# Attention scores: the second rotary product of four key tiles as one burst of half-height matmuls

## The chip, the cores and the metric

The kernel runs on one core of a Trainium2 chip. The metric is device time of one execution, in microseconds (us). The core has five engines that run side by side, each with its own queue: TensorE (PE, matmuls; its weight loads are listed as PEld), VectorE (DVE), ScalarE (ACT), GpSimd (POOL), and SyncE (SP), which issues transfers here. TensorE writes only to PSUM, which has 8 banks of 128 partitions x 512 float32 numbers.

## The reference

One layer of an encoder with two groups of heads: four heads of gated linear attention and four heads of multi-head latent attention. Their outputs are concatenated, projected, added to the input and normalised. The change lies in the softmax attention of the second group:

```python
s = (jnp.einsum('bqhd,bkhd->bhqk', qn, k_nope)      # 128 numbers per head
     + jnp.einsum('bqhr,bkr->bhqk', qr, k_r))       # 64 rotary numbers, one key for all heads
p = jax.nn.softmax(s, axis=-1)
return jnp.einsum('bhqk,bkhv->bqhv', p.astype(v.dtype), v)
```

The sequence has 2048 positions, so each of the four heads has a 2048 x 2048 table of scores. Inputs and output are float32.

## The kernel before

**Numbers in two parts.** TensorE multiplies a rounded type, `float32r`. To keep accuracy the kernel splits each operand into a high part (a rounding copy, `hi`, L397) and a low part (the rest, `lo`, L404), and a product is a sum of three: high x high, high x low, low x high (`mm3`, L452).

**Stages.** Up to about 607 us the kernel does the input projection and the linear attention, and lays out keys and queries. The scores run from 607.9 to 1084 us. After that come the rest of the last block and the output projection with the normalisation, up to the end. The prediction is about the middle stage, `attention` (L1606).

**Blocks and steps.** The attention works through 16 blocks; block i is one head and 512 queries. A block has 8 steps; step j handles a pair of key tiles, 2j and 2j+1, of 128 keys each. The keys lie along the partitions and the queries along the free dimension, so a pair of tiles gives 128 x 1024 scores in two PSUM banks, one for each tile (`e` = 0, 1 in the code).

**`scores(i, j)`** (L1632) issues five matmuls for each tile into its bank: high key x high query (L1640), high x low (L1641), low x high (L1642), and two for the rotary part (L1643, L1644). The rotary key has only 64 numbers, so its high part lies in rows 0 to 63 of a tile `kr` and its low part in rows 64 to 127; the rotary query is loaded twice, into both halves of 128 rows. A matmul over all 128 rows thus gives (high key + low key) x the query's high part `rh` (L1643), and a second one the same for its low part `rl` (L1644).

**The rest of a step**, each on its own engine:

| function | engine | does |
|---|---|---|
| `copy` (L1646) | ACT | scores from PSUM to SBUF |
| `smax` (L1651) | DVE | running maximum `rm`; for pair 0 one instruction (L1659) that reads bank and copy, else two (L1662) |
| `sub`, `exp` (L1683, L1688) | DVE, ACT | subtract the maximum `mb`, exponential, in place |
| `phi`, `plo` (L1692, L1697) | ACT, POOL | high and low part of the weights |
| `acc0`, `acc` (L1702, L1707) | ACT, DVE, POOL | sums over keys, for the denominator |
| `pv` (L1720) | PE | six matmuls with the values into the output bank `o` |

Once for each block: `tmax` (PE turns `rm` over into `mx`), `rmax` (DVE reduces it), `bmax` (PE spreads it over all partitions, `mb`); `tot`, `own_half` and `fold` close the sums, `tsum` and `rcp` invert them, `oh`, `ol`, `y` and `yc` turn `o` into the head's output.

**PSUM.** There are two score buffers of two banks (`pS`), so step j reuses what step j-2 had, once its copy and its maximum are done. The output `o`, the maxima, the turned-over tiles and the sums (`ap`) have one bank each. So `pv` of pair 0 waits for `oh` and `ol` of the block before, and `acc0`, which opens new sums, waits for the `fold` of the block before its own.

**The order is written out by hand.** Every call gets a place, in units of a step: step j of block i has t = 8i + j, and the dictionary `PLACE` (L79) gives the offset of each function, one number or one for each j. All calls are sorted by place (L1890), and every engine works in exactly that order (`in_order`, L416). An engine whose next instruction waits does not go on to a later one. Around the change the places, counted from the start of a block (mod 8), are:

- PE: step 0, `mx` 0.26, PV of pair 4 (of the block before) 0.27, `mb` 0.48, step 1, PV 5, step 2, PV 6, PV 7, step 3, the sums turned over (3.37), step 4, PV 0 at 4.35, step 5, PV 1, PV 2, step 6, step 7, `y` 7.55, PV 3.
- DVE: maximum of pair 7 at 0.21, `rmax` 0.27, maximum of pair 0 at 1.21, subtraction of pair 2 at 1.39, of 0 at 1.47, of 1 at 1.65, `tot` 2.2, maximum 1 at 2.21, subtraction 3 at 2.37, `fold` 2.95, maximum 2 at 3.21, subtractions 4 and 5, `ol` 3.99, maximum 3 at 4.21.
- ACT: copy of pair 0 at 0.73, high part 7 at 1.47, exponential 2 at 1.63, copy 1 at 1.73, exponential 0, high part 0, `own_half` 2.7, copy 2 at 2.73, `acc0` 2.78, exponential 1 at 2.95, `oh` 3.34, high part 1, copy 3 at 3.73.

The last block has places of its own (`PLACE_LAST`) for what comes after the maxima; the copies take theirs from `PLACE` in all blocks.

Of the kernel before, what the change touches and what calls it, by code (L numbers as in the profile page):

```python
# [76 lines left out]


PLACE = dict(  # L79
    copy=0.73,  # L80
    max=1.21,
    sub=(9.47, 8.65, 7.39, 7.37, 7.49, 6.63, 6.95, 7.44),
    exp=(10.18, 9.95, 7.63, 9.15, 8.26, 9.12, 7.84, 8.01),
# [9 lines left out]
    half=11.7,  # L93
# [51 lines left out]
    last=dict(P1=0.0, P5=2.72, P6=5.44, P3=8.16, P2=10.88, P7=13.6, P4=16.32),  # L145
# [244 lines left out]
class K:  # L390
# [1024 lines left out]

    def c_krsh(self, d):
        d["krs"] = self.w1.tile([P, 2, 64], F32R, tag="krs", name=f"krs{d['c']}")
        self.hi(d["krs"][:, 0], d["kr"][:, 0])

    def c_krsl(self, d):  # L1420
        self.lo(d["krs"][:, 1], d["kr"][:, 0], d["krs"][:, 0], "pool")

    def c_vh(self, d):
        self.hi(self.vh[:, d["c"]], d["ckv"])
# [181 lines left out]
    def attention(self):  # L1606
        tc, nc = self.tc, self.nc
        mm = nc.tensor.matmul
        V, G, Ac = nc.vector, nc.gpsimd, nc.scalar
        NP = NKT // 2  # L1610
        with ExitStack() as ctx:
# [20 lines left out]
            def scores(i, j):  # L1632


                d = stt[i]
                qh, ql, rh, rl = d["q"]
                ps = d["ps", j] = pS.tile([P, 2, QB], F32, tag="pS", name=f"pS{i}_{j}")
                for e in range(2):
                    kh, kl, kr = (t[:, 2 * j + e] for t in (self.ckvT_h, self.ckvT_l, self.kr))
                    mm(ps[:, e], kh, qh, start=True, stop=False)  # L1640
                    mm(ps[:, e], kh, ql, start=False, stop=False)  # L1641
                    mm(ps[:, e], kl, qh, start=False, stop=False)  # L1642
                    mm(ps[:, e], kr, rh, start=False, stop=False)  # L1643
                    mm(ps[:, e], kr, rl, start=False, stop=True)  # L1644

            def copy(i, j):  # L1646
                d = stt[i]
# [193 lines left out]
            for i in range(nb):  # L1841
                for j in range(NP):
                    t = NP * i + j
                    put(t, scores, i, j)
                    for n, f in (("copy", copy), ("max", smax), ("sub", sub), ("exp", exp), ("hi", phi), ("lo", plo),
                                 ("pv", pv), ("acc", acc)):
                        if n != "acc" or j != SUM_POOL[0] or i == nb - 1:
                            put(t + at(n, i, j), f, i, j)
                put(NP * i + at("acc0", i), acc0, i)
                for n, f in (("tmax", tmax), ("rmax", rmax), ("bmax", bmax)) + {nb - 1: (), nb - 2: own_late}.get(i, own):  # L1850
                    put(NP * i + NP - 1 + at(n, i), f, i)
                if i + 2 < nb:
                    put(NP * i + 4.05, fetch, i + 2)
# [35 lines left out]
            last = {}  # L1889
# [67 lines left out]
            half = 5.44  # L1957
            put(4 * half - 0.01, op.pair_banks)
            for c in (6, 7):
                o, t = rest[c], 2 * half * (c - 6)  # L1960
# [463 lines left out]
```

## Time and profile before

| | us |
|---|---|
| median of 3 runs | 1282.82 |
| lowest, highest | 1281.37, 1285.22 |
| the profiled execution | 1283.54 |
| its span (first to last instruction) | 1281.7 |

| engine | share of the span that it is busy | in one attention block of 30.93 us |
|---|---|---|
| PE | 98% | 30.93 |
| DVE | 73% | 27.59 |
| ACT | 68% | 25.85 |
| POOL | 67% | 26.20 |

How to read the rows: a row in order of time gives the start (us from the start of the span), the duration, the engine, the line of the kernel, the operation, what it writes and reads, shapes, and how many like it follow each other (xN); in square brackets stands how long the engine stood idle before it and which instruction released it. Matmuls overlap: the next one starts before the end of the record. A row of groups gives, after the bar, busy time, mean duration in ns, and the idle time ahead with its releaser. A row of stretches gives, for a stretch of time, its length and the busy time of each engine with the number of its instructions, then the granted clock of TensorE, the share of the DMA engines, and GB/s.

### The profile page before, as it was taken

Reading aid. Unit: us, or ns where it says so; the run is one execution under the profiler, and the core shown is the slowest. Engines: PE = TensorE matmul, PEld = TensorE weight load, DVE = VectorE, ACT = ScalarE, POOL = GpSimd, SP = SyncE. Lnnn points to the kernel's source line nnn. Section 1 sums busy time; section 2 is a strip of 40 time slices with the busy share of each in tenths; the row PEclk is TensorE's granted clock in tenths of the full one; section 3 lists DMA queues with packets and bytes.
Section 4 is the critical chain, followed back from the end, with each engine's and each line's share of the span. In section 5 each row is a group of like instructions: output and inputs, shape, how many; then the busy total and the mean of one; then the engine's idle time right before and its main releaser. Section 6 shows DMA issues by size and latency. Waiting matters only on the chain.

```text
span 1281.7 us, 20184 instructions
## 1 busy us (share of the span) xinstructions
PE 1255.0 (98%) x6928; PEld 1108.3 (86%) x6928; DVE 941.1 (73%) x1702; ACT 876.2 (68%) x1553; POOL 852.7 (67%) x550
## 2 busy tenths in 40 slices
PE   7999999999999999999999999999999999999996
PEld 7999999999889999999788888888888888788875
DVE  7865775656675445555798888888888889648887
ACT  7765657666675665665588888888888888623355
POOL 0245555363657666672188888889999999955784
PEclk9999999999999999999999999999999999999999
DMA  8332525253675565555501111122213221468962
GB/s 299 98 92 63 177 71 172 87 155 101 195 244 159 180 225 189 181 194 166 175 1 41 42 42 41 42 58 58 59 58 91 53 52 33 173 211 304 343 196 84
DMA packets 122518, 166.81 MB, mean 130 GB/s; under 512 B 18502, under 2 KB 71118, under 8 KB 121776
## 3 DMA queue, kind: packets, MB, share of 16 engines
q1 hardware_dynamic: 114256, 163.39, 40.2%
q0 software_dynamic: 768, 2.10, 0.5%
q8 instruction: 55, 0.90, 0.4%
q10 hardware_dynamic: 7392, 0.03, 0.3%
q14 instruction: 47, 0.39, 0.2%
HBM read 106.72 MB, written 58.75 MB: 129 GB/s over the span
## 4 chain that ended last, share of the span: by engine, by line
PE 75%; DVE 6%; ACT 5%; POOL 4%; DMA 3%; issue 3%; SPq 0%; DVEq 0%; POOLq 0%; ACTq 0%
PE pS L1640 4%; PE pS L1641 4%; PE pS L1642 4%; PE pS L1643 4%; PE pS L1644 4%; PE o L454 4%; PE o L455 4%; PE o L456 4%; PE ipa L454 3%; PE ipa L456 3%; PE ipa L455 3%; PE pz L455 2%; PE pz L456 2%; PE pz L454 2%; PE ipg L454 2%
## 5 line engine op out<-in xcount | busy, mean ns | idle before, releaser
L406 POOL TENSOR_TENSOR pl<-s,ph 128x1024 fp32r<-128x1024 f32 x128 | 306.3, 2417 | 56.3 <-ACT ph L400 56.3
L1662 DVE TENSOR_TENSOR rm<-pS,rm 128x512 f32<-128x512 f32 x210 | 144.8, 690 | 26.4 <-ACT s L1649 20.8
L1686 DVE TENSOR_TENSOR s<-s,mb 128x1024 f32<-128x1024 f32 x128 | 151.3, 1214 | 9.4 <-PE mb L1680 9.3
L1649 ACT ACTIVATE s<-pS 128x1024 f32<-128x1024 f32 x128 | 131.3, 1026 | 37.7 <-PE pS L1644 33.4
L400 ACT ACTIVATE ph<-s 128x1024 fp32r<-128x1024 f32 x128 | 134.9, 1057 | 13.5 <-PE o L456 12.7
L1690 ACT ACTIVATE s<-s 128x1024 f32<-128x1024 f32 x128 | 131.5, 1050 | 13.4 <-DVE s L1686 13.3
L454 PE MATMUL ipa<-wah,xah 128*128 128x384 f32 (+1 forms) x384 | 129.8, 338 | 6.3 <-ACT wah L400 6.3
L1103 POOL TENSOR_TENSOR Us<-Us,cw 128x512 f32<-128x512 f32 x16 | 18.6, 1164 | 173.4 <-DVE Us L1101 157.9
L456 PE MATMUL ipa<-wah,xal 128*128 128x384 f32 (+1 forms) x384 | 124.8, 325 | 0.0
L455 PE MATMUL ipa<-wal,xah 128*128 128x384 f32 (+1 forms) x384 | 124.5, 324 | 0.1
L1640 PE MATMUL pS<-qh,ckvT_h 128*128 128x512 f32 x256 | 102.6, 401 | 0.8 <-DVE rm L1662 0.4
L454 PE MATMUL o<-ph,vh 128*128 128x512 f32 x256 | 101.1, 395 | 0.0
L1641 PE MATMUL pS<-ql,ckvT_h 128*128 128x512 f32 x256 | 99.9, 390 | 0.0
L1642 PE MATMUL pS<-qh,ckvT_l 128*128 128x512 f32 x256 | 99.9, 390 | 0.0
L1643 PE MATMUL pS<-rh,krs 128*128 128x512 f32 x256 | 99.8, 390 | 0.0
L1644 PE MATMUL pS<-rl,krs 128*128 128x512 f32 x256 | 99.8, 390 | 0.0
L456 PE MATMUL o<-ph,vl 128*128 128x512 f32 x256 | 99.8, 390 | 0.0
L455 PE MATMUL o<-pl,vh 128*128 128x512 f32 x256 | 99.7, 390 | 0.0
L1713 DVE TENSOR_TENSOR ap<-ap,s 128x512 f32<-128x512 f32 x120 | 83.1, 693 | 3.5 <-ACT s L1690 0.9
L454 PEld LDWEIGHTS ipa<-wah,xah 128*128 128x128 f32 x384 | 73.0, 190 | 7.1 <-ACT wah L400 6.5
L454 PE MATMUL pz<-xch,wzh 128*128 128x256 f32 x256 | 74.8, 292 | 0.0
L455 PEld LDWEIGHTS ipa<-wal,xah 128*128 128x128 f32 x384 | 73.0, 190 | 1.2 <-DVE wal L406 0.6
(446 smaller groups left out, 3902.2 us busy)
## 6 DMA issues: line engine op xcount, KB each, us to landing
xcf<-xT_dram SPq DMA_DIRECT2D x16, 512.0 KB, 4.7
xr<-x_dram SPq DMA_DIRECT2D x16, 512.0 KB, 6.3
xaf<-xT_dram SPq DMA_DIRECT2D x14, 512.0 KB, 3.8
wb<-wO_dram SPq DMA_DIRECT2D x16, 256.0 KB, 3.0
oib<-oi_s SPq DMA_DIRECT2D x16, 256.0 KB, 3.7
qdb<-qd_s SPq DMA_DIRECT2D x16, 256.0 KB, 4.8
SU<-su_s SPq DMA_DIRECT2D x16, 256.0 KB, 4.6
ub<-u_s SPq DMA_DIRECT2D x16, 256.0 KB, 4.2
```

Of the source, the lines that this page charges most:

```text
L400: return nc.scalar.activation(dst, src, AF.Copy).ins
L406: return e.tensor_tensor(dst, src, hi.bitcast(F32), ALU.subtract).ins
L454: mm(out, ah, bh, start=start, stop=False)
L455: mm(out, ah, bl, start=False, stop=False)
L456: mm(out, al, bh, start=False, stop=stop)
L1640: mm(ps[:, e], kh, qh, start=True, stop=False)
L1641: mm(ps[:, e], kh, ql, start=False, stop=False)
L1642: mm(ps[:, e], kl, qh, start=False, stop=False)
L1643: mm(ps[:, e], kr, rh, start=False, stop=False)
L1644: mm(ps[:, e], kr, rl, start=False, stop=True)
L1662: V.tensor_tensor(d["rm"], src[:, e], d["rm"], ALU.max)
L1686: V.tensor_tensor(s, s, d["mb"][:, None, :].to_broadcast([P, 2, QB]), ALU.subtract)
```

## The change

`scores` no longer issues L1644 for each tile. In every odd step, ahead of its own matmuls, stands a burst of four matmuls over 64 rows: the second rotary products of the two tiles of the even step before (their last products), and those of the two tiles of this step (their first, which now open the banks). The tile of `e` = 0 uses rows 0 to 63 of key and query, that of `e` = 1 rows 64 to 127. These rows hold the key's high part alone: so that they do, tiles with an odd number now have high and low part of the rotary key the other way round (`c_krsh`, `c_krsl`; the transposition takes both along). The product of the key's low part with the query's low part is left out of the scores. An even step has 8 matmuls left, an odd step 8 and the burst.

The scores of an even pair are complete only after the first half of the burst in the next step, so the even copies get the place 1.002, right behind that step. All other places stay.

```diff
 PLACE = dict(
-    copy=0.73,
+    copy=(1.002, 0.73, 1.002, 0.73, 1.002, 0.73, 1.002, 0.73),
...
     def c_krsh(self, d):
         d["krs"] = self.w1.tile([P, 2, 64], F32R, tag="krs", name=f"krs{d['c']}")
-        self.hi(d["krs"][:, 0], d["kr"][:, 0])
+        self.hi(d["krs"][:, d["c"] % 2], d["kr"][:, 0])
 
     def c_krsl(self, d):
-        self.lo(d["krs"][:, 1], d["kr"][:, 0], d["krs"][:, 0], "pool")
+        p = d["c"] % 2
+        self.lo(d["krs"][:, 1 - p], d["kr"][:, 0], d["krs"][:, p], "pool")
...
                 ps = d["ps", j] = pS.tile([P, 2, QB], F32, tag="pS", name=f"pS{i}_{j}")
+                odd = j % 2
+                if odd:
+                    for t, last in ((j - 1, True), (j, False)):
+                        for e in range(2):
+                            half = slice(64 * e, 64 * e + 64)
+                            mm(d["ps", t][:, e], self.kr[half, 2 * t + e], rl[half], start=not last, stop=last)
                 for e in range(2):
                     kh, kl, kr = (t[:, 2 * j + e] for t in (self.ckvT_h, self.ckvT_l, self.kr))
-                    mm(ps[:, e], kh, qh, start=True, stop=False)
+                    mm(ps[:, e], kh, qh, start=not odd, stop=False)
                     mm(ps[:, e], kh, ql, start=False, stop=False)
                     mm(ps[:, e], kl, qh, start=False, stop=False)
-                    mm(ps[:, e], kr, rh, start=False, stop=False)
-                    mm(ps[:, e], kr, rl, start=False, stop=True)
+                    mm(ps[:, e], kr, rh, start=False, stop=bool(odd))
```

## The prediction

> **What bounds the kernel now.** I read the page first (busy shares, slices, groups), then the busy time in single attention blocks, then the order of time on each engine inside one block, and last the waits.
>
> ```profile
> span 1281.7 us, 20184 instructions
> PE 1255.0 (98%) x6928; PEld 1108.3 (86%) x6928; DVE 941.1 (73%) x1702; ACT 876.2 (68%) x1553; POOL 852.7 (67%) x550
> L1644 PE MATMUL pS<-rl,krs 128*128 128x512 f32 x256 | 99.8, 390 | 0.0
> ...
> core 0: us, PE busy (x) PEld busy (x) DVE busy (x) ACT busy (x) POOL busy (x), PEclk, DMA share, GB/s
> 715.73:746.66 30.93, 30.93 (x142) 25.54 (x141) 27.59 (x38) 25.85 (x30) 26.20 (x12) 1.00 0.17 44
> ```
>
> TensorE (PE) is busy 98% of the span, and in one attention block (715.73 to 746.66) for all of its 30.93 us, at full granted clock (1.00). So PE sets the pace of a block. But VectorE (DVE) has 27.59 us of work in the same block, only 3.34 us under it: what PE can give back is small before DVE, which also has to wait for others, takes over. The question is therefore what ordered waits DVE gets. Here is one block in order of time, DVE first, then ScalarE (ACT) with two rows of the waits of the attention (who waited for whom, us in total, times, longest), then PE.
>
> ```profile
> 718.63 0.69 DVE L1673 TENSOR_REDUCE mc<-mx 128x4 f32<-128x512 f32 x1 [0.87 <-PE mx L1668]
> 719.26 0.69 DVE L1659 TENSOR_TENSOR rm<-pS,s 128x512 f32<-128x512 f32 x1
> 720.54 3.48 DVE L1686 TENSOR_TENSOR s<-s,mb 128x1024 f32<-128x1024 f32 x3 [0.59 <-PE mb L1680]
> 723.94 1.43 DVE L1737 TENSOR_TENSOR ap<-ap,acc 128x512 f32<-128x512 f32 x2
> 725.27 1.41 DVE L1662 TENSOR_TENSOR rm<-pS,rm 128x512 f32<-128x512 f32 x2
> 726.60 1.21 DVE L1686 TENSOR_TENSOR s<-s,mb 128x1024 f32<-128x1024 f32 x1
> 727.82 0.85 DVE L1751 TENSOR_TENSOR acc<-ap,acc 64x256 f32<-64x256 f32 x2
> 728.71 1.42 DVE L1662 TENSOR_TENSOR rm<-pS,rm 128x512 f32<-128x512 f32 x2
> 730.04 2.34 DVE L1686 TENSOR_TENSOR s<-s,mb 128x1024 f32<-128x1024 f32 x2
> 732.30 0.69 DVE L406 TENSOR_TENSOR ofl<-o,ofh 128x512 fp32r<-128x512 f32 x1
> 732.90 1.41 DVE L1662 TENSOR_TENSOR rm<-pS,rm 128x512 f32<-128x512 f32 x2
> ```
>
> ```profile
> 718.20 1.03 ACT L1649 ACTIVATE s<-pS 128x1024 f32<-128x1024 f32 x1 [0.84 <-PE pS L1644]
> ...
> 726.59 1.03 ACT L1649 ACTIVATE s<-pS 128x1024 f32<-128x1024 f32 x1
> 728.77 0.60 ACT L1705 ACTIVATE ap<-s 128x512 f32<-128x512 f32 x1 [1.15 <-DVE acc L1751]
> 729.31 1.04 ACT L1690 ACTIVATE s<-s 128x1024 f32<-128x1024 f32 x1
> 730.26 0.58 ACT L400 ACTIVATE ofh<-o 128x512 fp32r<-128x512 f32 x1
> ...
> ACT ap L1705 <- DVE acc L1751: 15.2, 14, 1.2
> DVE rm L1662 <- ACT s L1649: 19.2, 28, 1.0
> ```
>
> ```profile
> 717.77 0.39 PE L1644 MATMUL pS<-rl,krs 128*128 128x512 f32 x1
> 718.00 0.60 PE L1668 MATMUL mx<-ident,rm 128*128 128x128 f32 x4
> 719.83 0.60 PE L1680 MATMUL mb<-ident,mc 128*128 128x128 f32 x4
> 720.50 0.40 PE L1641 MATMUL pS<-ql,ckvT_h 128*128 128x512 f32 x1
> ...
> 733.74 0.39 PE L454 MATMUL o<-ph,vh 128*128 128x512 f32 x1
> ...
> 735.10 0.39 PE L1640 MATMUL pS<-qh,ckvT_h 128*128 128x512 f32 x1
> ...
> 748.93 0.60 PE L1668 MATMUL mx<-ident,rm 128*128 128x128 f32 x4
> ```
>
> In the first fence DVE reduces the transposed maxima (718.63), takes key pair 0's maximum (719.26), then runs the subtractions of the block before without a gap up to the low part of the output (732.30, done 732.99). In the second, `acc0` (L1705) waits for DVE's fold (L1751), 14 times in the attention, and pair 2's copy (726.59) has already left **ahead** of it. The third gives PE's beat: six PV matmuls from 733.74 to 735.10, so 0.227 us each (a slot below), though a record is 0.39 long.
>
> **A closed loop in the block.** From `mx` (718.00) to the next `mx` (748.93) the engines release each other in a ring: `mx` to the first subtraction 720.54 - 718.00 = 2.54; the subtractions, `tot`, pair 1's maximum, the fold, up to pair 2's maximum 728.71 - 720.54 = 8.17; from there to the end of `ol` 732.99 - 728.71 = 4.28; then PV of pair 0, which needs `ol` because there is one output bank, and on PE to the next `mx`, 748.93 - 733.74 = 15.19. Sum 30.18; PV 0 starts 0.75 after `ol` is done, and 30.18 + 0.75 = 30.93. So DVE's ring has 0.75 us of slack in a block.
>
> **The change part by part.**
>
> *PE's work.* 256 second rotary products (L1644) become 64 bursts of four half-height ones. If two halves run side by side a burst has 2 slots in place of 4: 128 slots go, 29.1 us. No row of before has a half-height matmul, so a pair is bounded by one slot (side by side) and two (one after the other, no gain). I take side by side: the two halves share neither rows of the array nor a score bank. The second half's weights are a cost of their own:
>
> ```profile
> 1106.75 0.39 PE L456 MATMUL o<-ph,vl 128*128 128x512 f32 x1
> 1106.98 0.27 PE L1785 MATMUL rt<-ident,rc 128*4 128x128 f32 x1
> ...
> 1106.98 0.19 PEld L454 LDWEIGHTS o<-ph,vh 128*128 128x128 f32 x1
> 1107.09 0.19 PEld L455 LDWEIGHTS o<-pl,vh 128*128 128x128 f32 x1
> ```
>
> A weight load starts as the matmul before it starts (1106.98 and 1106.98), and the next can follow 0.11 later. So the second half lags the first by 0 (loaded ahead) to 0.11; I take 0.11, which is what these loads do. Saved on PE: 29.1 - 64 x 0.11 = 22.1 us. Changing the array's division costs, at both edges of a burst, between 0 and what a full run-out would: 0.39 - 0.227 = 0.16. The nearest row is the 4-column block, `rt`: it comes one ordinary slot after its predecessor (1106.75 to 1106.98) and the next load starts with it, so I take 0. The Trainium skill speaks against that: "TensorEngine Tiling (Array Packing)", Key Properties, says that a change of tiling mode drains the engine; by it the sum would be 1341 instead of 1329, and the `rt` row, which narrows columns and not rows, shows no such gap. "TensorE: Matmul & The Clock Gate", Part 3, gives about 4 ns of lag between packed tiles; by that the sum would be 1325, and no run here shows it yet.
>
> *The even pairs end later.* Their last product moves past everything that PE has between the two score steps: `mx`, PV 4 and `mb` for pair 0, PV 6 and 7 for pair 2, PV 0 for pair 4, nothing for pair 6. The even copies move from 0.73 to 1.002 in the order, the maxima stay at 1.21, the subtractions stay too. Two of these count.
>
> Pair 0: its maximum still stands ahead of the three subtractions on DVE. Now it needs the burst, which stands behind `mb`. From `mx`: 2.27 to the first slot after `mb` (720.50 - 0.23 = 720.27), 0.11 for the second half, 0.39 for the result, 0.04 to the copy (717.77 + 0.39 = 718.16 against 718.20), the copy 1.03, 0.03 to the maximum (719.23 against 719.26), the maximum 0.66 (725.27 to 726.60 for two): 4.53 in place of 2.54, **+1.99**. Queued behind it: all of DVE's subtractions, hence ACT's exponentials.
>
> Pair 2: its copy at 3.002 now stands behind `acc0` (2.78) and pair 1's exponential (2.95) on ACT, and `acc0` waits for the fold. So the copy starts where 730.26 stands, ends 1.03 later, and the maximum, 0.03 behind the copy, starts at 731.32 and not 728.71: **+2.61**. Queued behind it: two subtractions and `ol` on DVE, the score bank for step 4, and PV 0 on PE.
>
> Pair 4's copy and maximum (1.03 + 1.42) lie beside 8 slots of step 5 and 12 of PV 1 and 2 (4.5 us) before step 6 wants the bank; pair 6's beside 8 + 3 + 6 slots (3.9). Both hidden; without that cover each would cost up to its own 2.45. In PE's last leg four score steps lose 8 slots and two bursts bring 4 back: -4 x 0.227 + 2 x 0.11 = **-0.69**.
>
> *Swapping the order of high and low part by tile parity* (L1416 to L1421) keeps each instruction, its size and its queue; nothing moves, so it costs nothing, and no cover is needed. No DMA is added or moved.
>
> *The sum.* Ring after: 4.53 + 8.17 + 2.61 + 4.28 + (15.19 - 0.69) = 34.09 against PE's 30.93: +3.16 a block. It holds in the 14 blocks that have both the subtractions of the block before and the fold of the one before that; in the first two I take 1.5 together, between nothing and one full 3.16 (block 0 subtracts nothing, block 1 has no fold). 14 x 3.16 + 1.5 = 45.7. PE idles in these blocks, so its 22.1 us are gone inside the ring. What follows the scores has no such step and shifts as a whole. The profiled execution took 1283.54 us (span 1281.7), 0.7 above the median of 1282.82: 1283.5 + 45.7 = **1329 us**. Its own bounds: without the 0.11 (three in the ring) 14 x 0.33 less, 1325; with edges at 0.16 the 1341 below.
>
> **The rivals.**
>
> *The array's division costs, or the halves do not overlap.* Five edges lie in the ring (into the first burst, both of the third and fourth): 5 x 0.16 = 0.80. Halves one after the other (the change then does not do what it says): 0.12 on the first pair and 0.345 on two bursts, 0.81. Either gives 14 x 3.97 + 2 = 57.5: 1341. For it: no row shows half-height work. Against: `rt`. Both together: about 1352.
>
> *Only one of the two late copies counts.* If pair 2's is hidden, the ring is 31.48, 14 x 0.55 + 1 = 9: 1292. If pair 0's is, 32.10, 14 x 1.17 + 1 = 17: 1301. For it: ACT has 30.93 - 25.85 = 5.1 us of idle time. Against: both engines work in written order, and `acc0`'s wait stands in the trace.
>
> *Faster: PE stays the bound.* The ring stays below PE's own new time if the two extra waits (1.99 + 2.61) come, together, below 30.93 - 30.18 + 0.69 = 1.44 us a block; that is the point from which it decides. Then the 22.1 us arrive whole: 1283.5 - 22.1 = 1261 (1254 without the lag). The mechanism: DVE takes the late maxima from banks that were ready anyway, and its subtractions start at `mb` as now. For it: DVE's 3.34 us of air. Against: DVE idles 0.59 for `mb` now, with pair 0's maximum done; that maximum cannot precede a burst that stands behind `mb`.
>
> **How the numbers follow.** Forecast as summed: 0.55. Division or no overlap: 0.17. One late copy: 0.14. PE stays the bound: 0.10. No change: 0.04. A measurement of this kernel tells about 0.3% (4 us) from no change; the first three are slower: 0.86, faster 0.10, same 0.04. The range runs from the lower single-copy case less a microsecond, 1291, to the division case plus what the first two blocks may add, 1346; it leaves out the faster case, no change and both costs at once, 0.18. The likeliest alone: 1323 to 1332.
>
> **What would show it.** Right: blocks of about 34 us in the attention; DVE idle some 2 us ahead of L1659 with ACT's copy as releaser, and 2.6 ahead of pair 2's L1662, now after `acc0`; PE idle some 4 us a block ahead of step 4 and PV 0, released by DVE; the half products recorded with 64 rows, two starts 0.11 apart. Wrong: blocks under 30.9 with PE without a gap (faster), a maximum of pair 0 that starts after the subtractions, or gaps of 0.16 at each burst (division). The prediction falls if DVE's order is not that of the written places, or if `acc0` no longer waits for the fold.

## The result, and the profile after

| | before | after |
|---|---|---|
| median, us | 1283.01 | 1360.66 |
| lowest, highest | 1281.37, 1285.22 | 1357.49, 1362.39 |
| profiled execution, its span | 1283.54, 1281.7 | 1360.27, 1358.5 |

The ratio is 1.0601, with a 95% interval of 1.0576 to 1.0627: 77.7 us slower. The forecast was 1329, with a range up to 1346. The direction and the ring of waits were right, the size was not: two costs outside the ring's waits were missing.

The lines moved by six: L1644 is now the burst, L1647 to L1650 the four full-height products, L1655 the copy, L1665 and L1668 the maxima, L1692 the subtraction. First the page of the changed kernel, then two rows of busy time by stretch: 14 attention blocks, and 3.6 us out of one of them.

```profile
span 1358.5 us, 20129 instructions
PE 1281.3 (94%) x6928; PEld 1093.6 (81%) x6928; DVE 938.2 (69%) x1702; ACT 876.3 (65%) x1553; POOL 851.9 (63%) x550
PEclk9999999999999999999999998999989998999999
L1668 DVE TENSOR_TENSOR rm<-pS,rm 128x512 f32<-128x512 f32 x210 | 144.8, 690 | 76.0 <-ACT s L1655 71.3
L1647 PE MATMUL pS<-qh,ckvT_h 128*128 128x512 f32 x256 | 112.9, 441 | 46.4 <-DVE rm L1668 46.4
```

```profile
659.97:1164.09 504.12, 457.51 (x1974) 344.79 (x1973) 386.21 (x534) 367.49 (x416) 390.12 (x170) 0.95 0.16 42
784.80:788.40 3.60, 3.60 (x10) 2.79 (x11) 3.56 (x5) 3.58 (x4) 3.60 (x2) 0.57 0.00 0
```

Between the second `mx` and the last, 14 blocks take 504.12 us, 36.01 each; before it was 656.18 to 1088.01, 30.85 each. DVE's busy time in them is what it was (386.21, before 385.92), and PE, which had no gap, now idles 46.6 us. The granted clock is 0.95 in the mean, and 0.57 in the second row, which no forecast of mine contained.

DVE, ACT and PE of one block in order of time:

```profile
768.31 0.69 DVE L1679 TENSOR_REDUCE mc<-mx 128x4 f32<-128x512 f32 x1 [0.41 <-PE mx L1674]
771.65 0.69 DVE L1665 TENSOR_TENSOR rm<-pS,s 128x512 f32<-128x512 f32 x1 [2.65 <-ACT s L1655]
772.26 3.48 DVE L1692 TENSOR_TENSOR s<-s,mb 128x1024 f32<-128x1024 f32 x3
...
779.53 0.86 DVE L1757 TENSOR_TENSOR acc<-ap,acc 64x256 f32<-64x256 f32 x2
783.23 1.42 DVE L1668 TENSOR_TENSOR rm<-pS,rm 128x512 f32<-128x512 f32 x2 [2.85 <-ACT s L1655]
784.57 2.34 DVE L1692 TENSOR_TENSOR s<-s,mb 128x1024 f32<-128x1024 f32 x2
786.83 0.68 DVE L406 TENSOR_TENSOR ofl<-o,ofh 128x512 fp32r<-128x512 f32 x1
```

```profile
770.59 1.03 ACT L1655 ACTIVATE s<-pS 128x1024 f32<-128x1024 f32 x1 [3.10 <-PE pS L1644]
...
780.48 0.60 ACT L1711 ACTIVATE ap<-s 128x512 f32<-128x512 f32 x1 [2.31 <-DVE acc L1757]
781.10 1.06 ACT L1696 ACTIVATE s<-s 128x1024 f32<-128x1024 f32 x1
782.18 1.02 ACT L1655 ACTIVATE s<-pS 128x1024 f32<-128x1024 f32 x1
```

```profile
767.68 0.60 PE L1674 MATMUL mx<-ident,rm 128*128 128x128 f32 x4
769.49 0.60 PE L1686 MATMUL mb<-ident,mc 128*128 128x128 f32 x4
770.02 0.73 PE L1644 MATMUL pS<-rl,krs 64*128 64x512 f32 x4
770.68 0.50 PE L1647 MATMUL pS<-qh,ckvT_h 128*128 128x512 f32 x1
771.02 0.39 PE L1648 MATMUL pS<-ql,ckvT_h 128*128 128x512 f32 x1
...
781.24 0.38 PE L1769 MATMUL sx<-ident,acc 128*128 128x128 f32 x2
784.80 0.47 PE L1647 MATMUL pS<-qh,ckvT_h 128*128 128x512 f32 x1 [3.18 <-DVE rm L1668]
785.10 0.46 PE L1648 MATMUL pS<-ql,ckvT_h 128*128 128x512 f32 x1
785.36 0.63 PE L1649 MATMUL pS<-qh,ckvT_l 128*128 128x512 f32 x1
785.79 0.63 PE L1650 MATMUL pS<-rh,krs 128*128 128x512 f32 x1
...
787.92 0.63 PE L454 MATMUL o<-ph,vh 128*128 128x512 f32 x1
...
803.52 0.60 PE L1674 MATMUL mx<-ident,rm 128*128 128x128 f32 x4
```

Four things are to be seen. DVE idles 2.65 us for pair 0's copy ahead of its three subtractions. It idles 2.85 us for pair 2's copy, which stands behind `acc0` (L1711), which waits for the fold (L1757). The burst covers more than its own matmuls: its first one is recorded at 770.02, though the last `mb` slot ends at 769.49 + 4 x 0.11 = 769.93, and L1647's slot starts only 0.23 ahead of 771.02, at 770.79; from 769.93 to 770.79 are 0.86 us for four half products. And after a pause of 3.18 us PE's slots are 0.43 us long (785.36 to 785.79) where 0.23 is normal.

The weight loads show the edges of the burst:

```profile
769.27 0.58 PEld L1686 LDWEIGHTS mb<-ident,mc 128*128 128x128 f32 x4
770.02 0.30 PEld L1644 LDWEIGHTS pS<-rl,krs 64*128 64x128 f32 x4 [0.17 <-issue]
770.68 0.19 PEld L1647 LDWEIGHTS pS<-qh,ckvT_h 128*128 128x128 f32 x1 [0.36 <-issue]
770.79 0.19 PEld L1648 LDWEIGHTS pS<-ql,ckvT_h 128*128 128x128 f32 x1
```

No load is pulled ahead over a change of the array's division: each edge shows a pause that is put down to "issue" (0.17 and 0.36), and then the load itself lies open (0.11, 770.68 to 770.79).

### The profile page after: what moved, and what is told of

Same layout as the page of the kernel before. It is cut to its first block, busy times and chain, and to the rows that moved or that the text cites. A ratio compares the mean times of both kernels' runs of the same rounds, so it can differ in the third digit from the quotient of the medians.

```text
span 1358.5 us, 20129 instructions
## 1 busy us (share of the span) xinstructions
PE 1281.3 (94%) x6928; PEld 1093.6 (81%) x6928; DVE 938.2 (69%) x1702; ACT 876.3 (65%) x1553; POOL 851.9 (63%) x550
## 4 chain that ended last, share of the span: by engine, by line
PE 66%; DVE 14%; ACT 7%; issue 5%; POOL 3%; DMA 2%; SPq 0%; DVEq 0%; ACTq 0%; POOLq 0%
DVE s L1692 4%; PE pS L1647 4%; PE ipa L454 3%; PE ipa L456 3%; PE ipa L455 3%; PE o L454 3%; PE o L455 3%; PE pS L1648 3%; PE pS L1649 3%; PE o L456 3%; PE pS L1650 3%; DVE rm L1668 3%; ACT s L1655 2%; PE pz L455 2%; PE pS L1644 2%
## 5 line engine op out<-in xcount | busy, mean ns | idle before, releaser
L406 POOL TENSOR_TENSOR pl<-s,ph 128x1024 fp32r<-128x1024 f32 x128 | 306.0, 2402 | 131.9 <-ACT ph L400 126.0
L1655 ACT ACTIVATE s<-pS 128x1024 f32<-128x1024 f32 x128 | 131.2, 1025 | 103.9 <-PE pS L1644 78.9
L1668 DVE TENSOR_TENSOR rm<-pS,rm 128x512 f32<-128x512 f32 x210 | 144.8, 690 | 76.0 <-ACT s L1655 71.3
L1647 PE MATMUL pS<-qh,ckvT_h 128*128 128x512 f32 x256 | 112.9, 441 | 46.4 <-DVE rm L1668 46.4
L1692 DVE TENSOR_TENSOR s<-s,mb 128x1024 f32<-128x1024 f32 x128 | 151.1, 1212 | 1.2 <-PE mb L1686 1.2
L400 ACT ACTIVATE ph<-s 128x1024 fp32r<-128x1024 f32 x128 | 135.0, 1057 | 6.3 <-PE o L456 5.8
L454 PE MATMUL ipa<-wah,xah 128*128 128x384 f32 (+1 forms) x384 | 130.5, 340 | 7.2 <-ACT wah L400 7.2
L1647 PEld LDWEIGHTS pS<-qh,ckvT_h 128*128 128x128 f32 x256 | 50.2, 196 | 80.5 <-ACT ph L400 49.7
L454 PE MATMUL o<-ph,vh 128*128 128x512 f32 x256 | 105.1, 411 | 1.9 <-DVE ofl L406 1.9
L1649 PE MATMUL pS<-qh,ckvT_l 128*128 128x512 f32 x256 | 104.9, 410 | 0.0
L1648 PE MATMUL pS<-ql,ckvT_h 128*128 128x512 f32 x256 | 104.7, 409 | 0.0
L1650 PE MATMUL pS<-rh,krs 128*128 128x512 f32 x256 | 104.5, 408 | 0.0
L455 PE MATMUL o<-pl,vh 128*128 128x512 f32 x256 | 102.6, 401 | 0.0
L454 PEld LDWEIGHTS ipa<-wah,xah 128*128 128x128 f32 x384 | 73.5, 191 | 8.2 <-ACT wah L400 7.6
L454 PE MATMUL pz<-xch,wzh 128*128 128x256 f32 x256 | 74.8, 292 | 0.0
```

The lines of the kernel that those rows point to most:

```text
L400: return nc.scalar.activation(dst, src, AF.Copy).ins
L406: return e.tensor_tensor(dst, src, hi.bitcast(F32), ALU.subtract).ins
L454: mm(out, ah, bh, start=start, stop=False)
L455: mm(out, ah, bl, start=False, stop=False)
L1647: mm(ps[:, e], kh, qh, start=not odd, stop=False)
L1650: mm(ps[:, e], kr, rh, start=False, stop=bool(odd))
```

## The experiments

The theory after the result: two late copies in the ring (as predicted), 0.2 us at each edge of a burst, and a clock that is halved after the pause ahead of step 4. The experiments take these apart.

### One place: `acc0` behind pair 2's copy

```diff
-    acc0=10.78,
+    acc0=11.01,
```

> The changed kernel with one place moved: acc0 from 2.78 to 3.01, so that pair 2's copy stands ahead of it on ACT and no longer waits for the fold. Theory (two late copies in a ring, array edges of 0.2 us, and a halved TensorE clock after the 3.2 us stall ahead of step 4): the 2.6 us of DVE idle ahead of pair 2's maximum go, the stall ahead of step 4 falls under 1 us, the clock is no longer halved; blocks of 32 to 32.5 us instead of 36.0, about 1305 us. Rival (the half-height bursts themselves make up the time): less than 10 us better than 1361.

Measured: 1307.64 us, ratio to before 1.0191 (1.0169 to 1.0214); blocks of 32.4 us; granted clock 0.995. DVE of that kernel:

```profile
769.81 0.85 DVE L1757 TENSOR_TENSOR acc<-ap,acc 64x256 f32<-64x256 f32 x2
770.69 1.42 DVE L1668 TENSOR_TENSOR rm<-pS,rm 128x512 f32<-128x512 f32 x2
```

Pair 2's maximum follows the fold without a gap. One place in the order of ACT was worth 53 us of the 77.7, since with it the long pause of PE goes as well.

### The other place: pair 0's maximum behind the subtractions

```diff
-    max=1.21,
+    max=(1.7, 1.21, 1.21, 1.21, 1.21, 1.21, 1.21, 1.21),
```

> The changed kernel with one place moved: the maximum of pair 0 from 1.21 to 1.7, behind the three subtractions on DVE. Theory: the 2.65 us of DVE idle ahead of it go (about 2 us of them in the ring), pair 2's copy still waits for acc0 and the fold; the stall ahead of step 4 falls to about 1.2 us, too short to halve the clock; blocks of about 33 us, 1310 to 1318 us. Rival (only pair 2's copy counts): no better than 1345.

Measured: 1327.66 us, ratio 1.0347 (1.0323 to 1.0372); blocks of 33.75 us, clock 0.996. The gain is real (33 us), and the rival falls, but the number is off. The expectation took the whole 2 us out of the ring, though the maximum itself (0.61) is only moved to behind the subtractions, where it still stands ahead of pair 2's: from the first subtraction to pair 2's maximum it is 11.58 us in place of 10.97 (829.81 to 841.39).

### Both places

> Both places moved. Theory: the ring is back under 31 us and TensorE is the bound again; a burst takes 0.86 us where the four full-height products took 0.91, so blocks are 30.7 us and the time is 1278 to 1283 us, 0 to 5 below before. Rival (the bursts cost more than the records show, or the halves slow their neighbours): above 1290.

Measured: 1311.26 us, ratio 1.0221 (1.0204 to 1.0238). The expectation failed, and the number lies where the rival put it: with both orders mended the block is 32.7 us and no shorter than with `acc0` alone. But the cause is another one, as its ACT and DVE show:

```profile
766.96 1.03 ACT L1655 ACTIVATE s<-pS 128x1024 f32<-128x1024 f32 x1 [1.51 <-PE pS L1644]
```

```profile
765.32 0.85 DVE L1757 TENSOR_TENSOR acc<-ap,acc 64x256 f32<-64x256 f32 x2
768.02 1.42 DVE L1668 TENSOR_TENSOR rm<-pS,rm 128x512 f32<-128x512 f32 x2 [1.84 <-ACT s L1655]
```

Now the copy waits for PE itself: the burst that completes pair 2 stands behind PV 6 and PV 7. `mx` is at 754.92 in this block, so pair 2's maximum comes 13.10 us after it; before it was 728.71 - 718.00 = 10.71. A third path through the ring had lain hidden under the other two; the next experiment tests it.

### PV of pair 7 moved too

```diff
-    max=(1.7, 1.21, 1.21, 1.21, 1.21, 1.21, 1.21, 1.21),
+    max=(1.6, 1.21, 1.21, 1.21, 1.21, 1.21, 1.21, 1.21),
-    pv=(12.35, 12.1, 11.89, 12.65, 12.27, 12.25, 12.14, 11.45),
+    pv=(12.35, 12.1, 11.89, 12.65, 12.27, 12.25, 12.14, 12.2),
```

> Both places moved as before (pair 0's maximum at 1.6, acc0 at 3.01), and PV of pair 7 from 2.45 to 3.2, behind step 3, so that the burst that completes pair 2 comes 1.37 us earlier. Theory (with both queues free, what is left of 32.7 us a block is pair 2's data itself, which the burst completes only behind PV 6 and 7): blocks of 31.0 to 31.4 us, 1285 to 1292 us. Rival (the halved products slow the block wherever they stand): no better than 1305.

Measured: 1294.21 us, ratio 1.0086 (1.0069 to 1.0103). The rival falls. Most blocks take 31.3 us, four of the later ones 32.2, which is why the time lies 2 us above the range. In each of those four ACT has one instruction more ahead of pair 2's copy (the high part of the output weights, L400, 1.05 us), and the copy starts 11.5 us after `mx` there, 10.6 in the blocks beside them. So three moved places give back some 67 of the 77.7 us, the loss of clock included; that much came from the order in which late data meets the queues. What is left is still slower than before: PV 0 goes on waiting for `ol` (in the block from 813.50 the idle time ahead of PV 0 is 0.15 us, released by L406).

### The places of the copies alone, without the burst

```diff
 # in the kernel before
-    copy=0.73,
+    copy=(1.002, 0.73, 1.002, 0.73, 1.002, 0.73, 1.002, 0.73),
```

> The kernel before with the new places of the copies alone: no burst, no swapped parts, all products as before. Theory: pair 0's copy passes nothing and its scores are complete early, so it costs nothing; pair 2's copy stands behind acc0, which waits for the fold, and exp 1: +2.6 us against 0.75 of slack, so blocks of 32.8 us and about 1310 us. Rival (the late data of the burst, not the order, makes the wait): 1283 us as before.

Measured: 1318.24 us, ratio 1.0274 (1.0253 to 1.0294); blocks of 33.2 us. ACT and DVE:

```profile
769.94 0.60 ACT L1705 ACTIVATE ap<-s 128x512 f32<-128x512 f32 x1 [2.21 <-DVE acc L1751]
```

```profile
772.70 1.42 DVE L1662 TENSOR_TENSOR rm<-pS,rm 128x512 f32<-128x512 f32 x2 [2.85 <-ACT s L1649]
```

The same 2.85 us as in the changed kernel, though every product is in its old place: for pair 2's wait the order alone is enough. The 8 us above the expectation are about 0.4 us a block; the section on the prediction comes back to them.

### Is the divided array the cost? The burst at full height

```diff
                         for e in range(2):
-                            half = slice(64 * e, 64 * e + 64)
-                            mm(d["ps", t][:, e], self.kr[half, 2 * t + e], rl[half], start=not last, stop=last)
+                            mm(d["ps", t][:, e], self.kr[:, 2 * t + e], rl, start=not last, stop=last)
```

> The changed kernel with the burst as four matmuls over all 128 rows, same places: the late data and the late copies stay, the array is not divided. Theory (a burst of halves takes 0.86 us, of which 0.40 are its two edges; four full slots take 0.91): the time stays within 5 us of 1361. Rival A (the edges are what makes the change slow): 15 us or more better. Rival B (side by side, halves do save slots): 15 us or more worse.

Measured: 1358.88 us, against 1360.66 of the changed kernel. Four full slots and four halves with two edges cost the same; both rivals fall. The same pair was tried with the three places moved, where no clock is lost:

> The kernel with all three places moved (maximum of pair 0 at 1.6, acc0 at 3.01, PV 7 at 3.2; 1294 us) and the burst as four matmuls over all 128 rows. Theory (halves do run side by side, but a burst saves only 0.91 - 0.86 = 0.05 us): 0 to 4 us above 1294. Rival (dividing the array has a cost beyond its edges): faster than 1292.

Measured: 1295.36 us, ratio 1.0099 (1.0082 to 1.0115), blocks of 31.40 us against 31.33. That is the predicted side of zero, though the intervals overlap: the whole gain that the change could bring is some 3 us (64 x 0.05), if anything.

### The edges by themselves: two halves at the end of each step

```diff
 # in the changed kernel, copy=0.73 and no burst; for both tiles, then
+                for e in range(2):
+                    half = slice(64 * e, 64 * e + 64)
+                    mm(ps[:, e], self.kr[half, 2 * j + e], rl[half], start=False, stop=True)
```

> The halves issued in their own step, at its end, two for each step: no data is late, the copies keep the places of before, and there is a pair of edges in each of the 128 steps. Theory: TensorE stays the bound; a step has 8 slots, 0.20 + 0.23 + 0.20 us in place of 10 slots, so 0.18 us more a step, 22 us in all: 1305 us, score blocks of 32.3 us. Rival (edges hide under the run-out): 1283 or below.

Measured: 1304.94 us, ratio 1.0169 (1.0149 to 1.019), blocks of 32.3 us. PE has no gap between 660 and 1060 us, so this is a direct price. One step's end (L1644 is here the last full-height product, L1647 the two halves):

```profile
760.17 0.40 PE L1644 MATMUL pS<-rh,krs 128*128 128x512 f32 x1
760.49 0.51 PE L1647 MATMUL pS<-rl,krs 64*128 64x512 f32 x2
760.93 0.50 PE L454 MATMUL o<-ph,vh 128*128 128x512 f32 x1
761.26 0.40 PE L455 MATMUL o<-pl,vh 128*128 128x512 f32 x1
```

From the end of L1644's slot (760.40) to the start of L454's (761.26 - 0.23 = 761.03) are 0.63 us: one slot for two halves, and 0.20 at each edge. The two halves do run side by side: the records of both together are 0.51 long, hardly more than the 0.50 of the one after them.

### The clock: work for PE in the pause

```diff
                 # in tsum, after the transposes; nobody reads the product
+                if i < nb - 2:
+                    z = stt[i + 2]["q"][0][:, :2 * P]
+                    for n in range(24):
+                        mm(d["x"][:, 2:4].rearrange("p a t -> p (a t)"), self.ckvT_h[:, n % NKT], z, start=True, stop=True)
```

> The changed kernel with 24 matmuls of 256 columns, about 2.9 us, between the turned-over sums and step 4, where TensorE idles 3.2 to 3.5 us in each block; their product is read by nobody. Theory (the idle time halves TensorE's clock for some 3 us, which costs 1.2 us of the 36.0 in a block): no slots of 0.43 us after the stall, granted clock back near 1.00, blocks of 34.8 us and about 1344 us although PE has more to do. Rival (the slow slots have another cause, or the lost clock is off the ring): 1361 or more.

Measured: 1346.40 us, so 14.3 us **faster** with 336 matmuls more; blocks of 35.2 us, granted clock 0.997 (0.977 without).

```profile
778.43 3.10 PE L1773 MATMUL sx<-qh,ckvT_h 128*128 128x256 f32 x24
781.85 0.47 PE L1647 MATMUL pS<-qh,ckvT_h 128*128 128x512 f32 x1 [0.32 <-DVE rm L1668]
782.16 0.39 PE L1648 MATMUL pS<-ql,ckvT_h 128*128 128x512 f32 x1
782.39 0.40 PE L1649 MATMUL pS<-qh,ckvT_l 128*128 128x512 f32 x1
```

Step 4 waits for the same maximum as before, but its slots are 0.23 us from the second matmul on. The idle time itself was the cause.

> The changed kernel with 8 in place of 24 filling matmuls, so that TensorE idles some 2.4 us ahead of step 4 in place of 0.3 or 3.2. Theory (a pause this long already halves the clock, if less often): between 1347 and 1360 us with some slots of 0.43 us. Rival (only a pause of 3 us or more does): 1346 as with 24.

Measured: 1351.59 us, so the rival falls. With a pause of some 2.2 us (13 of the 14 are recorded as 2.18 to 2.23 us, one as 2.50, where the changed kernel has 3.16 to 3.45) the clock falls in some blocks and not in others, as two neighbours show:

```profile
735.15:770.30 35.15, 32.28 (x151) 24.44 (x150) 27.55 (x38) 25.79 (x31) 26.17 (x11) 1.00 0.16 47
770.30:806.45 36.15, 33.72 (x151) 25.29 (x150) 27.54 (x38) 25.81 (x31) 26.20 (x11) 0.95 0.12 30
```

A block with full clock takes 35.2 us, one with the slow stretch 0.6 to 1 us more. In the 14 blocks of the first three experiments and of the kernel with the places alone no pause is longer than 1.52 us, and the clock stays full there.

Which pauses are punished can be read from the changed kernel: the stretch of 3.41 us ahead of a slow one and the slow one itself, then a pair of stretches after which the clock stayed full.

```profile
781.87:785.28 3.41, 0.48 (x2) 0.47 (x3) 2.01 (x3) 3.39 (x5) 0.52 (x1) 1.00 0.00 0
785.29:788.70 3.41, 3.41 (x9) 2.63 (x9) 3.38 (x5) 3.09 (x4) 3.41 (x2) 0.50 0.00 0
747.74:751.15 3.41, 1.54 (x7) 1.33 (x8) 3.07 (x4) 3.41 (x5) 1.58 (x1) 1.00 0.00 0
751.15:754.56 3.41, 2.71 (x13) 1.44 (x11) 3.38 (x6) 2.05 (x3) 3.41 (x3) 1.00 0.00 0
```

All 12 slow stretches in the 14 blocks begin a whole number of times 3.413 us after the first of them, and each lasts 3.41 us or twice that. In the 3.41 us ahead of each PE idled for 1.93 us or more; in every other such stretch at full clock it idled for 1.87 us or less. The kernels with the full-height burst (1.93 against 1.84) and with 8 filling matmuls (1.96 against 1.68) divide in the same way. So in these traces it counts how much of a pause falls into one stretch of a fixed grid: a pause of 3.16 to 3.18 us that lay across two of them went unpunished twice. The border of 1.9 us holds for these blocks alone: at the start of the scores, ahead of them, 1.54 us of idling (pair 0's maximum moved), 1.79 (8 filling matmuls) and 1.81 (the places alone) were followed by a slow stretch too.

## Why the prediction was wrong

The ring of waits was the right picture, and its legs can be read off the quoted block:

| leg, us | before | predicted | measured | rows |
|---|---|---|---|---|
| `mx` to first subtraction | 2.54 | 4.53 | 4.58 | 767.68, 772.26 |
| to pair 2's maximum | 8.17 | 10.78 | 10.97 | 783.23 |
| to the end of `ol` | 4.28 | 4.28 | 4.28 | 787.51 |
| to PV 0 | 0.75 | 0 | 0.41 | 787.92 |
| PV 0 to next `mx` | 15.19 | 14.50 | 15.60 | 803.52 |
| block | 30.93 | 34.09 | 35.84 | |

**The two late copies** were sized right, each to within 0.2 us, and the experiments that take them out singly or make one alone confirm them. Nothing hid them, so the rivals "only one counts" and "PE stays the bound" fell.

**"Changing the array's division ... I take 0"** failed: it is 0.20 at each edge, where the range had 0.16 as its end, because besides the run-out the next weight load is not pulled ahead. The rival of a division that costs (1341) had this step right, with 0.16 for each edge. The row I leaned on, `rt`, narrows the weight block by columns and says nothing of rows. The "lag of 0.11" for the second half was wrong the other way: both halves' weights load together. Net, the first pair is ready 0.10 us later than summed (its copy starts 2.91 us after `mx`, where 2.81 stood) and two bursts take 0.30 more each, 0.70 a block, 10 us in all. The Trainium skill, "TensorEngine Tiling (Array Packing)", Key Properties, says that a change of mode drains the engine; the trace agrees, with 0.20 us at each edge.

**"PE idles in these blocks"** was written down and priced at nothing. This is the step that failed most: after a pause of 3.18 us the granted clock fell (0.57 over the next 3.6 us), step 4 and the start of PV 0 ran at half rate, and PV 0 came 0.41 us after `ol`. Filling the pause gives 14.3 us back. The Trainium skill, "TensorE: Matmul & The Clock Gate", Part 1, states that the clock is halved after an idle window of about 3.4 us, which runs free of the kernel's own time; the trace agrees on the half rate (0.43 against 0.23) and on a grid of 3.41 us that does not follow the kernel, but PE need not be idle for a whole one: 1.93 us of it were enough in these blocks, and pauses of 2.2 us.

**Smaller terms.** With the pause filled a block is 35.20: 34.09 + 0.70 leaves 0.41. Most of it can be read off the block of the filled kernel that starts at 764.72. From the start of `acc0` to the start of pair 2's copy ACT takes 1.70 us (777.53 to 779.23), where the rows of before that I put together have 1.49 (728.77 to 730.26); the same 1.70 stands in the changed kernel and in the one with the places alone, and why it is longer there is not shown. PV 0's first slot starts 0.17 after the end of `ol` (784.56 to 784.96 - 0.23), where I put nothing between them. The kernel with the places alone shows 0.4 as well. The first two blocks and what lies outside the 14 took 76.8 - 14 x 5.16 = 4.6 us, where 1.5 stood; with the pause filled 1.5 are left.

So, in us: 44 for the late copies as forecast, 10 for the edges, 14 for the clock, 6 for what else lengthened the ring, 2 for the rest: 76 of 77.7. The clock's 14 are the difference of two runs; the other terms are worked out from the rows of a block, times 14. The third path, pair 2's data behind PV 6 and 7, was missed in the prediction but cost nothing in this kernel; it decides only once the two orders are mended.

## What to carry to other kernels

When a change makes data late, price the instruction that waits for it by what stands behind it in its engine's written order, and by what now stands **ahead** of it: one copy that slipped behind a single waiting instruction cost more than all the matmuls in question. Close the ring of waits around a block and compare its length with that of the busiest engine; after mending one path, look for the next one under it. An engine that begins to idle may also become slower afterwards: here pauses of TensorE of 2.2 us had, in 6 of 14 blocks, a price beyond their own length, and pauses of up to 1.5 us had none.

## What was unexpected of the hardware

- Dividing the array into two halves of 64 rows, and joining it again, cost 0.20 us each way, so four half products (0.86 us) were hardly cheaper than four full ones (0.91), and two (0.63) dearer than two full ones (0.46); by these figures a burst would have to be longer to pay, which no run tried.
- Two half products with their own weights run side by side, weight loads included: the records of two pairs span 0.73 us, where four full ones take 0.91 in slots alone.
- Halved slots (0.43 us) followed 12 of the 14 long pauses of the changed kernel (3 to 12 slots each) and 6 of the 14 pauses of 2.2 us in the kernel with 8 filling matmuls (4 to 7 slots). In these blocks it went by how much of a pause fell into one stretch of a fixed grid of 3.41 us: 1.93 us or more was punished, 1.87 or less was not.
